# A transformer block on one core: forward sweeps half a step earlier, projections ahead of the scores, one bfloat16 product for a sum of squares

## The chip, the cores and the metric

The kernel runs on one core of a Trainium2 chip. The metric is the device time of one execution in microseconds (us). The engines are named as in the profile: PE multiplies matrices, PEld loads its weights, DVE, ACT and POOL do elementwise work, SP and ACT issue most of the DMAs.

## The reference

One diffusion-transformer block on x[2048, 1024], the first 256 rows of context apart. The input projection feeds eight heads of width 128: four of a gated linear recurrence (HGRN2) and four of retention. Each head runs over the sequence in both directions, its output is normalised per row, gated, and projected back; a gated feed-forward part with a three-tap convolution and a last normalisation follow.

```python
def step(r, inp):                                  # retention, per chunk of 64 rows
    qc, kc, vc = inp
    scores = jnp.einsum('bhtk,bhsk->bhts', qc, kc) * intra
    o = (jnp.einsum('bhts,bhsv->bhtv', scores, vc)
         + jnp.einsum('bhtk,bhkv->bhtv', qc * q_dec[:, :, None], r))
    r_new = (chunk_dec[:, None, None] * r
             + jnp.einsum('bhsk,bhsv->bhkv', kc * k_dec[:, :, None], vc))
    return r_new, o
```

HGRN2 has the same shape with a decay for every column and row in the place of `intra`. Retention's q and k are rotated first (`u1*cos - u2*sin`, `u1*sin + u2*cos`).

## The kernel before

**Products.** Every projection is a scheme of seven block products in the place of eight (`unit`: pa, pb, pa, pc, pa, pc, pa), and each block product is three float16 matmuls of high and low halves (`mm3`, L84 to L86). In the head stages a block product has 24 matmuls: `w_z` (q and k, or q and the forget gates) moves 256 columns per matmul, `w_vg` (values and output gate) 128. In the feed-forward part 512 columns move. After each block product ACT (L545, L547, L585) or DVE (L579) takes the result out of PSUM.

**Heads.** The tokens lie in four groups of 512. `heads()` walks 32 steps (h, i): head h of eight (0 to 3 HGRN2, 4 to 7 retention), group 3 - i. A step has two strands, which `weave` emits alternately: the main strand, `step(h, i)`, and a filler, the projection of the next step (18 block products for HGRN2, 14 for retention; 11 or fewer at the end). `weave` keeps the number of emitted filler pieces in proportion to the main strand's yields.

**Two sweeps.** `step(h, i)` runs the backward recurrence of head h over its group (`hg_sweep1` L809, with seven levels of scores `sc` L833 and DVE scaling L849 between them; or `ret_sweep1`), and beside it the forward recurrence of head h - 1, whose first sweep left all four groups behind. The forward sweep of group i has two parts. `hg_sweep2` or `ret_sweep2`: `fwd_state` makes four matmuls `o` (float32, L901), each followed by a DVE update of the state (L903); DVE adds `o` to the backward part (L928, L929 or L1236); `head_out` takes four sums of squares on ACT (L913), and `rstd` makes 1/sqrt of them in six small POOL instructions (`rs_v` to `rs_y`, L67 to L72). `hg_sweep2b` or `ret_sweep2b`: DVE scales the rows by that (L935 or L1243), four transposes on PE bring the result into `otp` (L920), ACT copies it, and a DMA writes it out. The first part is emitted at the start of the step, the second after the third yield of the main strand.

**Retention's rotation.** At the end of a step's filler for a retention head, ACT and DVE have written k and q side by side into one tile (shown as K). Four DMAs on ACT's queue (L1169) bring a copy with its 32-row blocks swapped (shown as Q). POOL multiplies the copy by sin (L1189), DVE multiplies K by cos (L1192) and adds both (L1193). The next step begins with the scores `rsc` (L1202), four float32 matmuls on that sum; DVE masks them (`rA`, L1204); transposes `rkp` (L1111), the increments `rup` (L1120), `rop` (L1215) and `rob` (L1222) follow.

**Upward weights.** In the feed-forward part `up_weights` is called 22 times. It loads two blocks of weights, takes their squares on ACT (L1478) into bfloat16, which also leaves the row sums in two columns `ssq`, multiplies the squares with a column of ones (16 matmuls of one column, `col`, L1483), and calls `allsum` (L102 to L108): one float32 matmul of one column per column of `ssq` with a square of ones (L107), which leaves the total on all partitions. `scales` (L649) makes the scale of the weights of it.

**Order.** The program is built with `tile.TileContext(nc, schedule_with_timeline_sim=True)`: each engine's order is set by the order of emission, moved by the scheduler's own estimate of when operands are ready. Every engine then executes its list in that order, and a wait holds up what stands behind it on that engine. One instruction (L1192) is held behind another by `issue_after`.

Of the kernel before, what the change touches and what calls it, by code (L numbers as in the profile page):

```python
# [11 lines left out]
BF16 = mybir.dt.bfloat16  # L12
# [3 lines left out]
ALU = mybir.AluOpType  # L16
PSUM = bass.MemoryType.PSUM

P = 128
# [4 lines left out]
NG = SEQ // G  # L24
CT = 256
NH = 4
# [20 lines left out]
def view(t, off, dims):  # L47
    return bass.AP(t.tensor, t.offset + off, [t.ap[0]] + dims)


class Kern:
# [50 lines left out]
    def allsum(self, cols, tag="tu"):  # L102

        o = self.ps(tag, [P, 1], "allsum")
        n = cols.shape[-1]
        for i in range(n):
            self.nc.tensor.matmul(o, self.onesq, cols[:, i:i + 1], start=i == 0, stop=i == n - 1, skip_group_check=True)  # L107
        return o  # L108

    def allmax(self, col, tag="tu"):  # L110
# [827 lines left out]
        nc.scalar.copy(m, tp.rearrange("p c t -> p (c t)"))  # L938
        nc.scalar.dma_start(self.mixd[h][:, g * G:(g + 1) * G], m)

    def weave(self, main, filler, n_main, n_fill):

        done = 0
        for j, _ in enumerate(main):
            while filler is not None and done * n_main < (j + 1) * n_fill:
                done += 1
                if next(filler, self) is self:
                    filler = None
        for _ in filler or ():
            pass  # L950

    def step(self, h, i, W, cur, prev, pr):

        pool = self.mp
        g = NG - 1 - i
        slot = i if h % 2 == 0 else NG - 1 - i
        hg, hgp = h < NH, h - 1 < NH
        if h < 2 * NH:
            main = (self.hg_sweep1 if hg else self.ret_sweep1)(pool, h % NH, g, slot, pr, cur)
        else:  # L960
            main = iter(())
        if prev is not None:
            (self.hg_sweep2 if hgp else self.ret_sweep2)(pool, (h - 1) % NH, i, prev)
        for j in range(3):
            next(main, None)
            yield
            if i == 0 and j == (1 if hg else 0) and h < 2 * NH:
                yield from (self.hg_context if hg else self.ret_context)(pool, h % NH, W, cur)
        if h or i:
            self.tick(self.n_tick)  # L970
        if prev is not None:
            (self.hg_sweep2b if hgp else self.ret_sweep2b)(pool, (h - 1) % NH, i, prev)
        yield from main
        if h or i:
            self.tick(self.n_tick)

    def heads(self):

        nc, pool = self.nc, self.mp
        W, items = self.W0, self.items0  # L980
        self.mod_first()
        items[5][0]()
        place = [self.gate_tile() for _ in range(4)]
        xc = self.load_rows(None, place)
        self.norm_rows(NG - 1, self.x3)
        for _, comp in items[:4]:
            comp()
        self.lower_bounds()
        self.mod1 = self.modulation(self.ep, pool, view(self.sv, V_N1, [[0, 2], [1, 8]]), self.modT[:, :, 8:16],
                                    self.modT[:, :, 0:8], 0, 1.3)  # L990
        ftags = "Kl", "Kl", "qf0", "qf1", "K0", "Q0"
        for _ in self.first_blocks(NG - 1, self.x3, self.places(ftags, "ftmp"), "pj", 1):
            pass
        for _, comp in items[4:]:
            comp()
        for w, dq in W.values():
            nc.vector.tensor_tensor(dq, dq, self.dqx[:, 0:1], ALU.mult)
        prev, items = None, []
        cur = dict(grp={}, sg={})
        pr = {}  # L1000
        first = self.hg_proj(pool, 0, NG - 1, W, pr, cur, True)
        zq = ("z",) * 7 + ("q",)
        rows = lambda g, tags: self.norm_rows(g, self.load_rows(g, [p() for p in self.places(tags, f"x{g}")]))
        x2 = rows(2, zq)
        for _ in self.with_blocks(first, self.first_blocks(2, x2, self.places(ftags, "ftmp"), "tu")):
            pass
        Wn = W
        for s in range(4 * 2 * NH):
            h, i = divmod(s, NG)
            hn, inn = divmod(s + 1, NG)  # L1010
            if i == 0:
                if h < 2 * NH - 1:
                    Wn, items = self.head_weights(h + 1)
                    n = -(-len(items) // 6)
                    if NH <= h < 2 * NH - 1:
                        mods = [it for c in ((4, 5, 6), (7, 8, 9), (10, 11))[h - NH] for it in self.mod_later(c)]

                        pairs = [items[k:k + 2] for k in range(0, len(items), 2)]
                        none = [(None, lambda: None)] * 2
                        items = []  # L1020
                        while pairs or mods:
                            items += (pairs.pop(0) if pairs else none) + (mods[:2] or none)
                            mods = mods[2:]
                        n = 4
                    self.todo += items
                else:
                    items = self.out_weights()
                    self.todo += items[:5]
                    n = 1
                self.n_tick = n  # L1030
            if i == NG - 1:
                while self.todo or self.loaded:
                    self.tick(4)
                if h == 2 * NH - 1:
                    self.todo += items[5:]
            blocks = None
            if s == 0:
                for _ in self.first_blocks(None, self.norm_rows(None, xc), self.places(("A", "A", "Ta", "Kl"), "cftmp", 2), "tu"):
                    pass
                blocks = self.first_blocks(1, rows(1, ("ou1", "ou2", "ou3", "q", "qf2")), self.places(zq, "ftmp"), "pj")  # L1040
            if s == 1:
                blocks = self.first_blocks(0, rows(0, ("ou2", "ou3", "qf2", "gate", "gate", "q")), self.places(zq, "ftmp"), "pj")
            if s == 4 * 2:
                self.ret_consts()
            prn = {}
            nxt = cur if inn else dict(grp={}, sg={})
            if hn < 2 * NH:
                filler = (self.hg_proj if hn < NH else self.ret_proj)(pool, hn % NH, NG - 1 - inn, Wn if inn == 0 else W, prn, nxt, *((True,) if blocks else ()))
                if blocks:
                    filler = self.with_blocks(filler, blocks)  # L1050
            else:
                filler = chain(self.ret_gate(NH - 1, 0, W, cur), self.ret_gate(NH - 1, 1, W, cur))
            self.weave(self.step(h, i, W, cur, prev, pr), filler, (14 if h < NH else 8) + (0 if i else 19 if h < NH else 10),
                       18 if hn < NH else 14 if hn < 2 * NH - 1 else 11 if hn < 2 * NH else 8)
            pr = prn
            if i == NG - 1:
                prev, W, cur = cur, Wn, nxt
        for i in range(NG):
            self.weave(self.step(2 * NH, i, None, None, prev, None), self.ret_gate(NH - 1, i + 2, W, prev) if i < 2 else None, 3, 4)
            if i == 1:  # L1060
                self.mixed_pairs(0)
# [402 lines left out]
    def up_weights(self, j, ty):  # L1464
# [10 lines left out]
        ssq = kp.tile([P, 2], F32, tag="ssqw2", bufs=2, name="ssqw")  # L1475
# [5 lines left out]
        for i in range(2):  # L1481
            for k in range(KT):
                nc.tensor.matmul(col[:, i:i + 1], sqs[i][:, k * P:(k + 1) * P], self.onesb, start=k == 0 and i == 0,  # L1483
                                 stop=k == KT - 1 and i == 1, skip_group_check=True)
        s, neg, dq = self.scales(self.allsum(ssq, "sc"), self.dqx[:, 1:2], ("dqz", "dqvg")[ty])

        if ty == 0:
            tap = kp.tile([P, 2, 3], F32, tag="taps", bufs=2, name="taps")
# [348 lines left out]
```

## Time and profile before

| | |
|---|---|
| device time, median of 3 runs | 2725.51 us (2723.41 to 2730.9) |
| device time of the profiled execution | 2735.92 us |
| span of the profiled execution | 2734.1 us |
| mean granted clock | 0.969 |
| PE busy | 2557.4 us (94%) |
| PEld busy | 1686.3 us (62%) |
| DVE busy | 1821.8 us (67%) |
| ACT busy | 1343.0 us (49%) |
| POOL busy | 779.3 us (29%) |

The busy times are unions of an engine's instruction intervals over the whole span; a PE that is busy is not PE at its highest rate, since its granted clock varies. By the trace, steps of HGRN2 heads fill about 270 to 800 us, steps of retention heads about 800 to 1300 us, and the upward part of the feed-forward about 1550 to 2263 us. The profiled execution was 10.4 us longer than the median run.

### The profile page before, as it was taken

Reading aid. Unit: us, or ns where it says so; the run is one execution under the profiler, and the core shown is the slowest. Engines: PE = TensorE matmul, PEld = TensorE weight load, DVE = VectorE, ACT = ScalarE, POOL = GpSimd, SP = SyncE. Lnnn points to the kernel's source line nnn. Section 1 sums busy time; section 2 is a strip of 40 time slices with the busy share of each in tenths; the row PEclk is TensorE's granted clock in tenths of the full one; section 3 lists DMA queues with packets and bytes.
Section 4 is the critical chain, followed back from the end, with each engine's and each line's share of the span. In section 5 each row is a group of like instructions: output and inputs, shape, how many; then the busy total and the mean of one; then the engine's idle time right before and its main releaser. Section 6 shows DMA issues by size and latency. Waiting matters only on the chain.

```text
span 2734.1 us, 56424 instructions
## 1 busy us (share of the span) xinstructions
PE 2557.4 (94%) x22829; PEld 1686.3 (62%) x22829; DVE 1821.8 (67%) x3569; ACT 1343.0 (49%) x2902; POOL 779.3 (29%) x905
## 2 busy tenths in 40 slices
PE   5788999999999999988999899999999999999998
PEld 2578888889888888887445344444444444444443
DVE  4988677776757565546464888877877777423553
ACT  4776456564544444435454566555555554411120
POOL 3733112220313132221244344334433433000101
PEclk6799999999999999999999999999999999999999
DMA  8224334243447676766631133333233234734552
GB/s 282 115 86 156 103 110 135 93 132 115 144 132 255 207 238 198 241 184 196 211 110 62 57 121 104 108 112 113 99 105 116 89 112 163 268 143 172 205 194 100
DMA packets 216694, 402.39 MB, mean 147 GB/s; under 512 B 16623, under 2 KB 98771, under 8 KB 211824
## 3 DMA queue, kind: packets, MB, share of 16 engines
q1 hardware_dynamic: 203808, 373.42, 39.8%
q10 hardware_dynamic: 12320, 25.18, 3.0%
q8 instruction: 179, 2.93, 0.4%
q14 instruction: 83, 0.68, 0.1%
q0 software_dynamic: 304, 0.17, 0.0%
HBM read 298.57 MB, written 91.75 MB: 143 GB/s over the span
## 4 chain that ended last, share of the span: by engine, by line
PE 61%; DVE 15%; DMA 8%; issue 7%; ACT 4%; POOL 4%; ACTq 1%; SPq 0%; POOLq 0%; DVEq 0%
PE pa L84 6%; PE pa L85 6%; PE pa L86 6%; PE pd L86 5%; PE pd L84 5%; PE pd L85 5%; DMA Q<-K 3%; PE pc L84 3%; PE pc L85 3%; PE pc L86 3%; PE pb L84 2%; PE pb L86 2%; PE pb L85 2%; PE opp L84 2%; PE opp L85 2%
## 5 line engine op out<-in xcount | busy, mean ns | idle before, releaser
L84 PE MATMUL pa<-feat,w 128*128 128x512 f16 x704 | 268.4, 381 | 14.2 <-ACT ta L545 9.8
L85 PE MATMUL pa<-feat,w 128*128 128x512 f16 x704 | 268.1, 381 | 0.0
L86 PE MATMUL pa<-feat,w 128*128 128x512 f16 x704 | 264.9, 381 | 0.0
L86 PE MATMUL pd<-wd,actl 128*128 128x512 f16 x616 | 233.5, 379 | 0.0
L85 PE MATMUL pd<-wd,actl 128*128 128x512 f16 x616 | 233.5, 379 | 0.0
L84 PE MATMUL pd<-wd,actl 128*128 128x512 f16 x616 | 232.8, 379 | 0.0
L85 PEld LDWEIGHTS <-w 128*128 128x128 f16 x1232 | 120.7, 98 | 156.8 <-issue 16.9
L86 PEld LDWEIGHTS <-w 128*128 128x128 f16 x1232 | 121.4, 99 | 145.3 <-issue 1.7
L84 PEld LDWEIGHTS <-w 128*128 128x128 f16 x1232 | 121.5, 99 | 141.4 <-issue 2.0
L85 PEld LDWEIGHTS <-hx 128*128 128x128 f16 x1824 | 182.0, 100 | 9.5 <-issue 7.3
L86 PEld LDWEIGHTS <-hx 128*128 128x128 f16 x1824 | 182.1, 100 | 2.8 <-issue 1.9
L84 PEld LDWEIGHTS <-hx 128*128 128x128 f16 x1824 | 182.4, 100 | 2.3
L1593 DVE SCALAR_TENSOR_TENSOR st<-act,modT,st 128x512 f16<-128x512 f32 x154 | 144.3, 967 | 32.1 <-ACT st L1592 32.1
L1592 ACT ACTIVATE st<-act,modT 128x512 f16<-128x512 f32 x154 | 107.3, 718 | 85.2 <-DVE act L1582 31.4
L84 PE MATMUL pa<-w_vg,hx 128*128 128x128 f16 x800 | 145.2, 222 | 2.9 <-DVE cb L579 2.3
L85 PE MATMUL pa<-w_vg,hx 128*128 128x128 f16 x800 | 144.9, 222 | 0.0
L86 PE MATMUL pa<-w_vg,hx 128*128 128x128 f16 x800 | 144.8, 222 | 0.0
L84 PE MATMUL pc<-feat,w 128*128 128x512 f16 x352 | 133.5, 379 | 1.2 <-ACT feat L1367 1.1
L86 PE MATMUL pc<-feat,w 128*128 128x512 f16 x352 | 133.5, 379 | 0.0
L85 PE MATMUL pc<-feat,w 128*128 128x512 f16 x352 | 133.5, 379 | 0.0
L84 PE MATMUL pa<-hx,w_z 128*128 128x256 f16 x464 | 127.7, 275 | 5.1 <-ACT ct L545 1.6
L85 PEld LDWEIGHTS <-w_z 128*128 128x128 f16 x1072 | 109.2, 102 | 36.4 <-issue 24.1
(550 smaller groups left out, 7563.0 us busy)
## 6 DMA issues: line engine op xcount, KB each, us to landing
hx<-hxd SPq DMA_DIRECT2D x212, 512.0 KB, 4.9
actd<-st SPq DMA_DIRECT2D x154, 256.0 KB, 2.0
actl<-actd SPq DMA_DIRECT2D x28, 1024.0 KB, 5.0
wur<-in_w_up_dram SPq DMA_DIRECT2D x44, 512.0 KB, 3.8
raw<-in_w_in_dram SPq DMA_DIRECT2D x36, 512.0 KB, 4.3
wm<-in_w_mod_dram SPq DMA_DIRECT2D x64, 256.0 KB, 3.8
hxd<-hx SPq DMA_DIRECT2D x28, 512.0 KB, 3.2
wdb<-in_w_down_dram SPq DMA_DIRECT2D x44, 256.0 KB, 4.0
```

The source lines that it names most:

```text
L84: mm(ps, lhs(0), rhs(0), start=start, stop=False, skip_group_check=True)
L85: mm(ps, lhs(0), rhs(1), start=False, stop=False, skip_group_check=True)
L86: mm(ps, lhs(1), rhs(0), start=False, stop=stop, skip_group_check=True)
L1592: nc.scalar.activation(p[:, 0], v, AF.Copy, scale=s)
L1593: nc.vector.scalar_tensor_tensor(p[:, 1], v, s, p[:, 0], ALU.mult, ALU.subtract)
```

## The change

There are three edits.

1. `step`: within a head, the forward sweep of group i + 1 is emitted in step i, its first part after the main strand's third yield, its second part at the end of the step. Group 0's sweep stays at the start of step 0, so that the last step of a head (i = 3) has no forward sweep of its own. The pass behind the last head is as before.
2. `weave` takes `lead`: with retention heads (h >= 4) two block products of the filler are emitted ahead of the main strand's first instruction, which is `rsc`.
3. `allsum16`: in `up_weights` DVE adds the two columns of `ssq` into one bfloat16 column (`both`, L113 of the new kernel), and one bfloat16 matmul (L115) takes the place of the two float32 ones. It is done 22 times: 44 float32 matmuls of one column go, 22 bfloat16 ones and 22 DVE additions come.

```diff
+    def allsum16(self, cols, tag):
+
+        both = self.wp.tile([P, 1], BF16, tag="both", bufs=2, name="both")
+        self.nc.vector.tensor_tensor(both, cols[:, 0:1], cols[:, 1:2], ALU.add)
+        o = self.ps(tag, [P, 1], "allsum")
+        self.nc.tensor.matmul(o, view(self.onesb, 0, [[0, P]]), both, start=True, stop=True, skip_group_check=True)
...
-    def weave(self, main, filler, n_main, n_fill):
-
-        done = 0
+    def weave(self, main, filler, n_main, n_fill, lead=0):
+
+        done = lead
+        for _ in range(lead):
+            next(filler)
...
-        if prev is not None:
-            (self.hg_sweep2 if hgp else self.ret_sweep2)(pool, (h - 1) % NH, i, prev)
+        if prev is not None and (last or i == 0):
+            other(sweep2, i)
         for j in range(3):
...
         if h or i:
             self.tick(self.n_tick)
-        if prev is not None:
-            (self.hg_sweep2b if hgp else self.ret_sweep2b)(pool, (h - 1) % NH, i, prev)
+        if prev is not None and (last or i == 0):
+            other(sweep2b, i)
+        ahead = prev is not None and not last and i + 1 < NG
+        if ahead:
+            other(sweep2, i + 1)
         yield from main
         if h or i:
             self.tick(self.n_tick)
+        if ahead:
+            other(sweep2b, i + 1)
...
-                       18 if hn < NH else 14 if hn < 2 * NH - 1 else 11 if hn < 2 * NH else 8)
+                       18 if hn < NH else 14 if hn < 2 * NH - 1 else 11 if hn < 2 * NH else 8, 2 if h >= NH else 0)
...
-        s, neg, dq = self.scales(self.allsum(ssq, "sc"), self.dqx[:, 1:2], ("dqz", "dqvg")[ty])
+        s, neg, dq = self.scales(self.allsum16(ssq, "sc"), self.dqx[:, 1:2], ("dqz", "dqvg")[ty])
```

**Place 1, POOL, steps of head 4.** `Q<-Q,sin` is the rotation's multiply of one group, the six `rs_` rows are the forward sweep's 1/sqrt of one group (here of head 3). Before:

```order
L1189 TENSOR_TENSOR Q<-Q,sin 128x1024 x2
L67 TENSOR_SCALAR rs_v<-ossq 128x4
L68 TENSOR_TENSOR rs_y<-rs_v,mhalf 128x4
L69 TENSOR_TENSOR rs_t<-rs_y 128x4
L70 TENSOR_TENSOR rs_t<-rs_t,rs_v 128x4
L71 TENSOR_SCALAR rs_t<-rs_t 128x4
L72 TENSOR_TENSOR rs_y<-rs_y,rs_t 128x4
```

The changed kernel at the same place:

```order
L1208 TENSOR_TENSOR Q<-Q,sin 128x1024
L67 TENSOR_SCALAR rs_v<-ossq 128x4
L68 TENSOR_TENSOR rs_y<-rs_v,mhalf 128x4
L69 TENSOR_TENSOR rs_t<-rs_y 128x4
L70 TENSOR_TENSOR rs_t<-rs_t,rs_v 128x4
L71 TENSOR_SCALAR rs_t<-rs_t 128x4
L72 TENSOR_TENSOR rs_y<-rs_y,rs_t 128x4
L1208 TENSOR_TENSOR Q<-Q,sin 128x1024
```

Two multiplies stood ahead of one group of six; now a group of six stands between them, and the two alternate through the steps of retention.

**Place 2, PE, the forward sweep of head 4, group 2 (step h = 5).** `o` are the sweep's matmuls, `rkp` the transposes behind this step's scores, `w_vg` and `hx` the filler. Before, behind the step's scores:

```order
L86 MATMUL pc<-w_vg,hx 128x128
L107 MATMUL allsum<-ssqw,ones 128x1
L901 MATMUL o_15654<-Sf,qf 128x128
L901 MATMUL o_15654<-ou,qf 128x128 x3
L1111 MATMUL rkp<-ident,K 128x128 x4
```

The changed kernel, ahead of the step's scores:

```order
L86 MATMUL pa<-w_vg,hx 128x128
L84 LDWEIGHTS hx
L84 MATMUL pa<-w_vg,hx 128x128
L909 MATMUL o_15381<-Sf,qf 128x128
L909 MATMUL o_15381<-ou,qf 128x128 x3
L85 LDWEIGHTS hx
L85 MATMUL pa<-w_vg,hx 128x128
```

The same four matmuls moved up by some 600 rows of PE's list, from behind the scores into the projection ahead of them. The transposes `otp` of that group moved up by less (from 203 rows behind the matmuls to 604).

**Place 3, PE and DVE, one sum in the upward stage.** `col` is the last of the 16 products with ones, `feat` and the `w` behind it are the projection. PE before:

```order
L1483 LDWEIGHTS w_27837
L1483 MATMUL col<-onesb,w_27837 128x1
L107 MATMUL allsum<-ssqw,ones 128x1 x2
L86 LDWEIGHTS w_27538
L86 MATMUL pb<-feat,w_27538 128x512
```

PE now:

```order
L1502 LDWEIGHTS w_27855
L1502 MATMUL col<-onesb,w_27855 128x1
L115 LDWEIGHTS onesb
L115 MATMUL allsum<-both,onesb 128x1
L84 LDWEIGHTS w_27555
L84 MATMUL pb<-feat,w_27555 128x512
```

DVE now, at the addition of the same sum:

```order
L1587 SCALAR_TENSOR_TENSOR act<-edge,taps,act 128x1
L1582 SCALAR_TENSOR_TENSOR act<-ta,taps,act 128x511
L1588 SCALAR_TENSOR_TENSOR act<-edge,taps,act 128x1
L113 TENSOR_TENSOR both<-ssqw 128x1
L587 TENSOR_TENSOR ta<-pc,ta 128x512
L1581 SCALAR_TENSOR_TENSOR act<-ta,taps,act 128x511
```

On PE the sum keeps its place behind the column products. On DVE the addition `both` stands ahead of the next evacuation of a projection block (`ta<-pc`).

## Rows read from the trace of the kernel before

**Rows 1.** Windows by stage (stretch, length, busy by engine, PEclk, DMA share, GB/s).

```profile
270.00:800.00 530.00, 493.73 (x8095) 443.62 (x8094) 372.35 (x843) 291.39 (x726) 99.16 (x113) 0.98 0.36 119
800.00:1300.00 500.00, 449.37 (x5257) 422.09 (x5257) 302.39 (x675) 223.90 (x565) 118.87 (x143) 0.96 0.66 213
1600.00:2300.00 700.00, 697.26 (x3518) 324.06 (x3517) 559.51 (x964) 408.17 (x717) 282.87 (x188) 1.00 0.31 106
```

**Rows 2.** Waits of PE, whole span (total us, times, longest us).

```profile
PE sc L833 <- DVE Q L849: 13.9, 4, 3.7
...
PE otp L920 <- DVE ou L1243: 12.9, 4, 6.7
...
PE otp L920 <- DVE ou L935: 10.2, 6, 3.0
...
PE rsc L1202 <- DVE K L1193: 7.8, 3, 3.2
...
PE rsc L1202 <- DVE p2t L97: 4.5, 1, 4.5
```

**Rows 3.** Timeline of PE, two waits of `otp` whose place changes little.

```profile
820.63 0.66 PE L920 MATMUL otp<-ident,ou 128*128 128x128 f32 x4 [1.49 <-DVE ou L935]
...
1046.95 0.85 PE L920 MATMUL otp<-ident,ou 128*128 128x128 f32 x3 [3.36 <-DVE ou L1243]
```

**Rows 4.** Timeline of PE at one sum of the upward stage (start, duration).

```profile
1691.45 0.47 PE L1483 MATMUL col<-onesb,w 128*128 128x1 bf16 x13
...
1691.78 0.59 PE L107 MATMUL allsum<-ssqw,ones 128*128 128x1 f32 x4
...
1692.23 0.38 PE L86 MATMUL pb<-feat,w 128*128 128x512 f16 x1
```

**Rows 5.** Timeline of DVE and ACT ahead of the same sum.

```profile
1688.85 0.69 DVE L579 TENSOR_TENSOR ta<-pc,ta 128x512 f32<-128x512 f32 x1 [2.41 <-ACT ta L545]
...
1689.89 0.19 ACT L1478 ACTIVATION_READ_ACCUMULATOR w<-wur 128x1 f32 x1
```

**Rows 6.** Timeline of the forward sweep of head 3, group 3 (step h = 4).

```profile
903.48 0.69 DVE L928 TENSOR_TENSOR ou<-ou,o 128x512 f32<-128x512 f32 x1 [0.83 <-PE o L901]
...
910.82 2.35 POOL L1189 TENSOR_TENSOR Q<-Q,sin 128x1024 f32<-128x1024 f32 x1 [20.52 <-DMA Q<-K]
...
913.25 0.19 POOL L67 TENSOR_SCALAR rs_v<-ossq 128x4 f32<-128x4 f32 x1
...
916.52 1.09 PE L920 MATMUL otp<-ident,ou 128*128 128x128 f32 x4 [2.98 <-DVE ou L935]
```

**Rows 7.** Windows behind three waits of PE (columns as in rows 1).

```profile
882.00:886.00 4.00, 4.00 (x36) 3.86 (x37) 4.00 (x6) 3.46 (x8) 3.00 (x2) 0.64 0.40 138
916.50:922.00 5.50, 5.47 (x32) 4.51 (x33) 5.37 (x13) 3.37 (x9) 0.00 (x0) 0.50 0.46 142
1111.00:1115.00 4.00, 4.00 (x19) 3.27 (x20) 2.19 (x4) 0.84 (x2) 0.00 (x0) 0.50 1.03 413
```

**Rows 8.** Timeline of one rotation and its scores (step h = 6, i = 2).

```profile
1093.99 0.46 ACT L585 ACTIVATE K<-pa,dqk 128x256 f32<-128x256 f32 x1
...
1106.10 3.38 POOL L1189 TENSOR_TENSOR Q<-Q,sin 128x1024 f32<-128x1024 f32 x1 [9.41 <-DMA Q<-K]
...
1110.80 2.08 PE L1202 MATMUL rsc<-K 128*128 128x128 f32 x8 [3.16 <-DVE K L1193]
```

**Rows 9.** Timeline of PE in that step: matmuls of 128, then 256 columns.

```profile
1105.05 0.22 PE L84 MATMUL pa<-w_vg,hx 128*128 128x128 f16 x1
...
1106.06 0.27 PE L84 MATMUL pb<-hx,w_z 128*128 128x256 f16 x1
...
1107.37 0.27 PE L86 MATMUL pa<-hx,w_z 128*128 128x256 f16 x1
```

**Rows 10.** Groups by line and form, DVE: one state update of a forward sweep.

```profile
L903 DVE SCALAR_TENSOR_TENSOR ou<-ou,T 128x128 f32<-128x128 f32 x32 | 11.1, 347 | 0.3
```

**Rows 11.** Timeline of DVE: a multiply that starts within POOL's.

```profile
851.39 3.21 DVE L1192 TENSOR_TENSOR K<-K,cos 128x1024 f32<-128x1024 f32 x1
```

More of the change, by code (lines that the diff above doesn't have):

```diff
@@ L107, in allsum @@
             self.nc.tensor.matmul(o, self.onesq, cols[:, i:i + 1], start=i == 0, stop=i == n - 1, skip_group_check=True)
+        return o
+    def allsum16(self, cols, tag):
[3 more added lines that the diff above has]
+        self.nc.tensor.matmul(o, view(self.onesb, 0, [[0, P]]), both, start=True, stop=True, skip_group_check=True)
         return o
@@ L957, in step @@
         hg, hgp = h < NH, h - 1 < NH
-        if h < 2 * NH:
+        last = h == 2 * NH
+        sweep2, sweep2b = (self.hg_sweep2, self.hg_sweep2b) if hgp else (self.ret_sweep2, self.ret_sweep2b)
+        other = lambda sweep, k: sweep(pool, (h - 1) % NH, k, prev)
+        if not last:
             main = (self.hg_sweep1 if hg else self.ret_sweep1)(pool, h % NH, g, slot, pr, cur)
@@ L966, in step @@
             yield
-            if i == 0 and j == (1 if hg else 0) and h < 2 * NH:
+            if i == 0 and j == (1 if hg else 0) and not last:
                 yield from (self.hg_context if hg else self.ret_context)(pool, h % NH, W, cur)
```

## The prediction

> **What bounds the kernel now.** I read the windows by stage first. In the upward stage PE is busy 697.3 of 700 us at a granted clock of 1.00, DVE 559.5 [rows 1]: what goes from PE there goes from the time. In the HGRN2 steps PE is busy 493.7 of 530 us and DVE 372.4, in the retention steps PE 449.4 of 500 and DVE 302.4 [rows 1]. There PE is the busiest engine, but it stops: what a change is worth is in the waits that end last. So I went on to the list of PE's waits. The transposes of a forward sweep, `otp`, wait 12.9 us for retention's scaled rows and 10.2 us for HGRN2's, ten times in all. The scores of retention, `rsc`, wait 7.8 us for the rotated k and q, and 4.5 us once for a late DVE instruction. The level scores `sc` of HGRN2 wait 13.9 us for DVE [rows 2]. These are the three places that the first two edits touch.
>
> The timeline of one sweep shows why `otp` waits. DVE adds the `o` products at 903.48, `otp` starts at 916.52: 13.0 us. Of these, POOL's six small instructions and DVE's scaling take only 916.52 - 913.25 = 3.3; they stood behind the rotation's multiply, which began at 910.82 when its DMA landed [rows 6]. PE had less than 13 us of other work in its list between the two and stopped for 2.98.
>
> A stop costs more than itself. Behind `otp` at 916.5 the granted clock is 0.50 for 5.5 us, that is 1.2 of 2.4 GHz; behind the stop that ended at 882 it is 0.64 on average over 4 us; behind the score wait that ended at 1110.8, 0.50 over 4 us [rows 7]. Before the fall PE had stood idle in each. At full speed the first two stretches would have taken 5.5 x 0.50 + 4 x 0.36 = 4.2 us less.
>
> **The sums (edit 3).** Two float32 matmuls take 1692.23 - 1691.78 = 0.45 us of PE. A bfloat16 matmul of one column takes (1691.78 - 1691.45) / 13 = 0.025 [rows 4]. The new sum is of the latter kind: 0.45 - 0.025 = 0.425 saved, 22 times **-9.3 us**. Bounds: 0 if PE waits for the operand as long, and -9.9 if even the new one is hidden. Its operand has a new step, DVE's addition `both`, which waits for ACT's sums of squares. ACT had them at 1690.08, PE's sum began at 1691.78 [rows 4, 5], and an addition of two columns is of the size of the smallest DVE instructions. So it comes in time. The addition now stands ahead of the evacuation `ta<-pc` that ran at 1688.85, and would hold it up by 1.2 us, after DVE had been idle for 2.41 [rows 5]. I cost that at nothing: DVE has 140 us to spare in the stage [rows 1], and the block that needs this PSUM bank again is a block product further.
>
> **The earlier sweeps (edit 1).** Four `o` matmuls, six to nine DVE instructions, four squares on ACT, six on POOL, four transposes, a copy and one DMA are moved, none added. I counted PE's instructions between `o` and `otp` in the new order. Prices: a matmul of 128 columns (1106.06 - 1105.05) / 18 = 0.056 us, of 256 columns (1107.37 - 1106.06) / 12 = 0.109 [rows 9]; a float32 one 2.08 / 4 at half clock, so 0.26 [rows 7, 8]. For head 4's group 2 there were 87, 12 and 12 of them, 9.3 us, and now there are 214, 84 and 12, 24.3 us: more than the 13.0 that the slow case of the chain took. Of the ten waits, seven rise like this (from 9 to 11 us of work to 15 to 41). Three don't: the one in the last pass, 6.7, which the edit leaves alone [rows 2], head 3's group 0, 1.49, and head 4's group 3, 3.36 [rows 3], where the distance is as before (14.3 and some 10.2 us). So 12.9 + 10.2 - 6.7 - 1.5 - 3.4 = **-11.5 us** goes; bounds 0 and -16.4 (all but the last pass). On POOL a group of six now stands between each two multiplies, so that the six wait for at most one. Two sweeps, group 1 of heads 4 and 5, get shorter distances (17.3 to 10.1 us): without a multiply ahead of the six, 10 us suffice; with one, each stops for 2.9, which the range holds.
>
> The half-clock stretches at 882 and 916.5 follow two of the waits that go (head 3's groups 2 and 3): **-4.2 us**, bounds 0 and twice that.
>
> The output's copy and DMA move to the end of the step, behind the rotation's four DMAs on ACT's queue, and nobody reads them before the heads are done: nothing. ACT's squares come earlier among evacuations; ACT is busy 291.4 of 530 and 223.9 of 500 us [rows 1]: nothing.
>
> In HGRN2 the moved sweep's DVE work, four updates of 0.347 [rows 10] and two elementwise instructions like the 0.69 of [rows 6], 2.8 us, now falls among the levels of the step, where PE already waits for DVE [rows 2]. Nine sweeps of heads 0 to 2 move. Bounds: -13.9 if those waits vanish, as no sweep opens a step any more, and 9 x 2.8 = +25 if DVE sets the pace throughout. With DVE busy 70% I take a third of one sweep for each of the three heads, **+3 us**, near the row of mean use.
>
> **The lead (edit 2).** From the last q-and-k product to the scores the chain takes 1110.80 - 1093.99 = 16.8 us in one step, of which PE waited 3.16 [rows 8]. In the new order 16 matmuls of 128 columns and 12 of 256 fewer stand between: 0.9 + 1.3 = 2.2 us less cover, and so +2.2 in this step and in the like one of head 5. The 4.5 us wait of head 7's last step [rows 2] gains 4.9 us of cover and goes. Two steps (first of heads 5 and 6) fall from 19 or more to 15 us: +2 each if the chain is as long there. Head 7's first wait loses 1. Together 4.4 - 4.5 - 1 + 4 = **+3 us**; bounds -12.3 (all score waits gone) and +7 with half clock behind two of them.
>
> **Sum.** -9.3 - 11.5 - 4.2 + 3 + 3 = -19. The profiled execution was 2735.9 (span 2734.1 and 1.8 around it), 10.4 above the median of 2725.5. Against the median: **2706 us**. About 0.3%, 8 us, is what a measurement of this kernel can tell from no change.
>
> **Rivals.**
>
> *A, the rotation sets the pace.* The score chain runs through DMA, POOL and DVE and takes its 17 us whether PE is early or not. What the sweeps give back in the retention steps is then waited for at `rsc`: the 2.98 of [rows 6], at most as much for the stop at 882, 12.9 - 6.7 - 3.4 = 2.8 of retention's own, and 4.2 of clock, 13 in all. For it: [rows 8]. Against: only four of sixteen score groups wait now [rows 2]. 2706 + 13 = 2719, 2712 if half.
>
> *B, the sums gain nothing.* `both` sits behind long DVE work, or holds up `ta<-pc` until PE stops. For it: 1.2 us late at its place. Against: the 2.41 us of idle DVE just there [rows 5]. 2706 + 9.3 = 2715.
>
> *C, slower: DVE is the bound among HGRN2's levels.* All nine moved sweeps cost their 2.8 us, +25 in the place of +3, and behind every second the clock falls for 2.1 us (half of the 4.2 above), +9. 2706 - 3 + 25 + 9 = 2737. It decides from the point where a moved sweep costs PE over 2.4 us: (2733.7 - 2703 - 9) / 9. For it: `sc` waits for DVE now [rows 2]. Against: DVE's 372 of 530 us [rows 1].
>
> *D, DVE and POOL block each other.* POOL's multiply takes 2.35 us in [rows 6] and 3.38 in [rows 8], where DVE's multiply had started just before; DVE's takes 3.21 when it starts within POOL's [rows 11]. The moved sweeps of retention, twelve, come nearer to the multiplies; if each meets one and adds 3.38 - 2.35 = 1.03, +12: 2718. Against: most of the moved DVE work lies 7 to 12 us from the multiply in the new order. The Trainium skill, "SBUF — State Buffer", section "Who interferes with whom", says that a DVE instruction with two SBUF inputs and a POOL instruction that reads SBUF exclude each other for a whole instruction, whichever starts first; by that rule such meetings would be paid in full, and the durations here agree in kind.
>
> **Chances.** The forecast 0.60 (2692 to 2717); A 0.17; B 0.07; C 0.10; D 0.06. Faster by over 0.3% (under 2717.3): all of the forecast, 0.05 of A, 0.04 of B, 0.69. Within 0.3%: the rest of A and B, D and a hundredth of C, 0.22. Slower: 0.09. The range, 2690 to 2726, takes in A, B, D and most of the forecast's bounds, and leaves out C and the tail of large gains.
>
> **What would show it.** Right: `otp` waits of about 11 us in all, nearly all in the last pass and two others; the upward stage 9 us shorter with PE as full as before; no stretch of 0.50 at the steps of head 4's groups 2 and 3. A shows as more `rsc` waits on `K`, with longer idle time of POOL for the DMA. B shows as waits of `allsum` for `both`, or of block products for `ta`. C shows as `sc` waits well above 13.9 us and a longer HGRN2 stage. D shows as multiplies above 2.35 us and state updates above 0.35. I am wrong if the upward stage is not shorter, or if the head stages together do not gain.

## The result, and the profile after

The changed kernel takes **2707.65 us** (median of 4 runs, 2706.15 to 2709.88) against 2724.46 for the kernel before, measured beside it (median of 4, 2720.33 to 2730.9). The ratio is 0.994, with a 95% interval of 0.992 to 0.9961: 10.6 to 21.8 us less. The forecast was 2706, 19 us less, within 2690 to 2726.

The windows by stage of the changed kernel, cut as in [rows 1] and with the same columns:

```profile
270.00:800.00 530.00, 496.89 (x8160) 447.36 (x8158) 371.18 (x857) 292.14 (x728) 97.87 (x113) 0.99 0.37 120
800.00:1300.00 500.00, 456.51 (x5295) 421.39 (x5294) 311.67 (x683) 230.71 (x580) 123.88 (x155) 0.97 0.68 219
1600.00:2300.00 700.00, 699.49 (x3497) 320.88 (x3496) 569.68 (x995) 402.32 (x705) 278.61 (x184) 1.00 0.33 113
```

These windows hold more work than those of before, since the stages begin earlier in them. PE is fuller in all three, and the granted clock is 0.01 higher in the two head stages. To compare like with like, the stages have to be cut at instructions. The timeline of PE of the changed kernel has these starts: the fourth `uf` (an HGRN2 step), the first scores of retention, the first product of the output projection, the first column sum of the upward stage, and the first downward product.

```profile
302.34 1.16 PE L877 MATMUL uf<-V,KTt 128*128 128x128 f32 x8
...
791.90 1.06 PE L1221 MATMUL rsc<-K 128*128 128x128 f32 x8
...
1276.40 0.63 PE L84 MATMUL opp<-wo,mp 128*128 128x512 f16 x1
...
1418.02 0.54 PE L1502 MATMUL col<-onesb,w 128*128 128x1 bf16 x16
...
2298.06 1.03 PE L84 MATMUL pd<-wd,actl 128*128 128x512 f16 x4
```

Their differences give the stages HGRN2 (489.6), retention (484.5), output (141.6) and upward (880.0). The same cuts in the profile of every kernel of this study, in us:

| kernel | edits | HGRN2 | retention | upward |
|---|---|---|---|---|
| before | none | 495.3 | 499.6 | 886.8 |
| after | 1, 2, 3 | 489.6 | 484.5 | 880.0 |
| e1_sums | 3 | 495.8 | 493.2 | 875.7 |
| e2_sweeps | 1 | 492.2 | 488.7 | 884.8 |
| e3_lead | 2 | 493.8 | 498.9 | 884.6 |
| e4_sweeps_lead | 1, 2 | 490.4 | 489.7 | 886.4 |
| e5_hg_only | 1 in HGRN2 steps | 490.0 | 493.4 | 886.9 |
| e6_ret_only | 1 in retention steps | 495.8 | 488.9 | 885.9 |
| e7_no_lead | 1, 3 | 489.6 | 490.6 | 880.6 |
| e8_rot_dve | multiply on DVE | 495.0 | 485.9 | 886.6 |
| e9_all_rot | 1, 2, 3, multiply on DVE | 488.8 | 491.7 | 879.1 |
| e10_sums_rot | 3, multiply on DVE | 497.5 | 484.4 | 879.4 |
| e11_no_lead_rot | 1, 3, multiply on DVE | 489.7 | 489.4 | 875.2 |
| e12_hg_sums_rot | 1 in HGRN2 steps, 3, multiply on DVE | 489.3 | 477.5 | 881.0 |

The table also shows what one profile is worth. The HGRN2 column falls into two groups that do not overlap, 493.8 to 497.5 without early sweeps there (six kernels, mean 495.5) and 488.8 to 492.2 with them (eight, mean 489.9). In retention the code of before and of e1_sums is the same, and their profiles differ by 6.4. So of the 26 us between the two profiled spans (2734.1 and 2708.1), where the medians differ by 16.8, some 9 are not the change's; the ratio is the measure of the whole.

PE's waits in the whole span of the changed kernel (total us, times, longest):

```profile
PE sc L841 <- DVE Q L857: 11.1, 6, 3.7
PE otp L928 <- DVE ou L1262: 11.0, 6, 7.0
...
PE rsc L1221 <- DVE K L1212: 6.9, 5, 2.5
...
PE col L1502 <- ACT w L1497: 5.0, 3, 2.7
...
PE otp L928 <- DVE ou L943: 2.9, 2, 2.3
```

Against [rows 2], `otp` waits for the sweep's DVE rows fall from 23.1 to 13.9 us. 8.0 of that is in the last pass (the forward sweep of head 7), where 6.7 stood; everywhere else they fall from 16.4 to 5.9. `rsc` falls from 12.3 to 6.9, `sc` from 13.9 to 11.1. A wait of `col` for ACT's squares, 5.0 us, is new.

### The profile page after: what moved, and what is told of

The parts are those of the page before. It is cut to its first block, busy times and chain, and to the rows that moved or that the text cites. A ratio compares the mean times of both kernels' runs of the same rounds, so it can differ in the third digit from the quotient of the medians.

```text
span 2708.1 us, 56296 instructions
## 1 busy us (share of the span) xinstructions
PE 2538.8 (94%) x22763; PEld 1669.8 (62%) x22763; DVE 1827.9 (67%) x3591; ACT 1342.9 (50%) x2902; POOL 780.4 (29%) x905
## 3 DMA queue, kind: packets, MB, share of 16 engines
q1 hardware_dynamic: 203808, 373.42, 40.2%
## 4 chain that ended last, share of the span: by engine, by line
PE 65%; DVE 15%; DMA 6%; issue 5%; POOL 4%; ACT 4%; ACTq 0%; DVEq 0%; SPq 0%; POOLq 0%
PE pa L84 7%; PE pa L85 7%; PE pa L86 7%; PE pd L86 5%; PE pd L84 5%; PE pd L85 5%; PE pc L84 3%; PE pc L86 3%; PE pc L85 3%; PE pb L84 2%; PE pb L85 2%; PE pb L86 2%; DMA Q<-K 2%; PE opp L86 2%; PE opp L85 2%
```

## The experiments

**Each edit alone, and the first two together.** The four were measured on one chip, beside the same 31 runs of the kernel before.

e1_sums is the kernel before with this line and the new function only:

```diff
-        s, neg, dq = self.scales(self.allsum(ssq, "sc"), self.dqx[:, 1:2], ("dqz", "dqvg")[ty])
+        s, neg, dq = self.scales(self.allsum16(ssq, "sc"), self.dqx[:, 1:2], ("dqz", "dqvg")[ty])
```

> The kernel before with the new sums alone (edit 3). Theory 1, PE is full in the upward stage and each sum gives back 0.425 us: 9.3 us faster than before (ratio 0.9966), at most 10. Theory 2, the operand that DVE adds comes late or holds up DVE, and the gain is lost: within 2 us of before (ratio 0.999 to 1.001).

Measured: ratio 0.9957 (0.9942 to 0.9972), 11.7 us less on 2730.5. Theory 1; the predicted 9.3 lies inside the interval, theory 2 far outside.

e2_sweeps has the new `step`, with the old sums and without the lead:

```diff
+        if ahead:
+            other(sweep2, i + 1)
         yield from main
         if h or i:
             self.tick(self.n_tick)
+        if ahead:
+            other(sweep2b, i + 1)
```

> The kernel before with the earlier forward sweeps alone (edit 1). Theory 1, the waits of otp go and nothing takes their place: 11.5 + 4.2 - 3 = 12.7 us faster (ratio 0.9953). Theory 2, the retention steps are bound by the rotation's chain, and what otp gives back is waited for at rsc as long as no projection product stands ahead of it: within 4 us of before (0.9985 to 1.0), rsc waits of some 15 us in all in the place of 12.3.

Measured: 0.9965 (0.9954 to 0.9976), 9.6 us less. That is three quarters of theory 1's 12.7, which lies at the interval's edge (12.6); theory 2 is out.

e3_lead has the lead alone:

```diff
-                       18 if hn < NH else 14 if hn < 2 * NH - 1 else 11 if hn < 2 * NH else 8)
+                       18 if hn < NH else 14 if hn < 2 * NH - 1 else 11 if hn < 2 * NH else 8, 2 if h >= NH else 0)
```

> The kernel before with the two projection products ahead of the scores alone (edit 2). Theory 1, the prediction's term: 3 us slower to no change (1.000 to 1.001). Theory 2, the products cover the rotation's chain: the 12.3 us of rsc waits mostly go, 6 to 12 us faster (0.9955 to 0.998).

Measured: 1.0016 (1.0005 to 1.0027), 4.4 us more. Theory 1 has the sign, but not the reason. PE's waits in this run:

```profile
PE otp L928 <- DVE ou L1253: 15.7, 5, 6.5
...
PE otp L928 <- DVE ou L943: 9.2, 7, 2.4
...
PE otp L928 <- DVE modT L243: 5.5, 2, 3.0
...
PE rsc L1212 <- DVE p2t L97: 2.9, 1, 2.9
PE rsc L1212 <- DVE K L1203: 2.2, 3, 1.1
```

The score waits did fall, from 12.3 to 5.1 us, as theory 2 says, and `otp` rose to 30.4 us, from 23.1 in [rows 2] and 1.5 more on `modT`. So with sweeps that start late, two products ahead of the scores mostly move the stop. Together these waits fall by 1.4 us, though, and the profiled run (2730.8 us) is one of the fastest of its twelve (median 2734.5): where the 4.4 us go is not shown.

e4_sweeps_lead is both:

> Earlier sweeps and lead, with the old sums (edits 1 and 2). Theory 1: 12.7 - 3 = 9.7 us faster (0.9964), so that the sums add 9.3 to it in the changed kernel. Theory 2, only the two together help: 9 us faster or more here, though the runs with each alone show little.

Measured: 0.9961 (0.995 to 0.9972), 10.6 us less, theory 1's 9.7 within it. Beside the early sweeps the lead moves the time by 0.0004, which the intervals cannot tell from nothing.

**Where the early sweeps gain.** A switch limits the early order to some steps. The next four kernels were measured on one chip, beside the same 23 runs of before.

```diff
+        early = h < NH
...
-        if prev is not None and (last or i == 0):
+        if prev is not None and (not early or i == 0):
...
-        ahead = prev is not None and not last and i + 1 < NG
+        ahead = prev is not None and early and i + 1 < NG
```

> The kernel before with earlier sweeps in the steps of HGRN2 heads alone (heads 0 to 2 swept early, 9 sweeps). Theory 1, as the prediction has it: three small otp waits go (3.2 us) and DVE's levels take about as much back: 0.999 to 1.001. Theory 2, the gain of edit 1 lies here: 6 us or more faster (under 0.998). Theory 3, DVE is the bound among the levels: slower, over 1.002.

Measured: 0.9986 (0.9977 to 0.9995), 3.8 us less, between theories 1 and 2. The HGRN2 stage is 5.5 us under the mean of the late kernels. PE's waits in that stage, before:

```profile
PE sc L833 <- DVE Q L849: 10.2, 3, 3.4
...
PE otp L920 <- DVE ou L935: 3.2, 3, 1.9
PE sf L840 <- DVE Q L849: 2.8, 1, 2.8
PE kp L864 <- DVE K L844: 1.9, 2, 1.4
```

and in the changed kernel (in e5_hg_only the same three rows read 9.0, 3.1 and 1.1):

```profile
PE sc L841 <- DVE Q L857: 7.4, 5, 2.0
...
PE kp L872 <- DVE K L852: 3.1, 2, 1.6
...
PE sf L848 <- DVE Q L857: 1.1, 1, 1.1
```

The window of the stage, columns as in [rows 1], before:

```profile
302.00:797.30 495.30, 463.96 (x7633) 417.18 (x7632) 346.56 (x794) 271.73 (x683) 90.93 (x108) 0.98 0.37 120
```

and after:

```profile
302.30:791.90 489.60, 461.42 (x7632) 415.23 (x7632) 341.51 (x794) 271.44 (x683) 89.64 (x108) 0.99 0.37 122
```

All three `otp` waits are gone, and of `sc` and `sf` 4.5 us too; `kp` took 1.2. As many matmuls kept PE busy 2.5 us less, as the granted clock is 0.99 in the place of 0.98. So the levels' waits on DVE became shorter, not longer. DVE's busy time in the stage fell by 5.0 us with as many instructions: single ones became shorter, above all the 72 scalings of the levels (58.8 us before, 55.5 now). Why they did stays open.

For e6_ret_only the switch reads `early = NH <= h < 2 * NH`.

> The kernel before with earlier sweeps in the steps of retention heads alone (heads 3 to 6 swept early, 12 sweeps). Theory 1: otp waits of 8 us and their half-clock stretches go, 8 to 12 us faster, nearly all of what edit 1 alone gave (0.9965): 0.9956 to 0.997. Theory 2, given back at rsc: within 3 us of before (0.999 to 1.0).

Measured: 0.999 (0.9981 to 0.9998), 2.7 us less: theory 1 is out, and theory 2's bounds hold. Its waits in the retention stage:

```profile
PE otp L928 <- DVE ou L1263: 10.4, 5, 6.9
PE rsc L1222 <- DVE K L1213: 6.8, 6, 3.0
...
PE allsum L107 <- ACT wo L1304: 4.6, 1, 4.6
PE rsc L1222 <- DVE p2t L96: 3.7, 1, 3.7
...
PE otp L928 <- DVE ou L943: 1.8, 2, 1.2
```

`otp` outside the last pass stands at 4.6 us in the place of 13.2 ([rows 2] less the 3.2 of HGRN2). But 10.5 us of `rsc` waits stay, and an `allsum` of the output weights (`wo`) waits 4.6 us for ACT, which no list of before shows. The time between the first scores of one head and the next tells where it goes: head 4 took 125.7 us before and 122.1 here; head 5 128.5 and 119.1 (from 922.9 to 1051.4 and from 919.9 to 1039.0); head 6 took 121.9 before, 117.6 in e1_sums and 122.9 here; head 7 to the output projection 123.6, 121.7 and 124.8. The gain comes in heads 4 and 5. That part of it goes back in heads 6 and 7 is not shown, since before and e1_sums, with the same retention code, lie over 4 us apart in head 6. The two halves together, 3.8 + 2.7, are less than the 9.6 of edit 1 in one piece, though their intervals (up to 6.3 and 5.2) allow it; that they help each other was not shown.

e7_no_lead is the changed kernel without the lead.

> The changed kernel without the two products ahead of the scores (edits 1 and 3). Theory 1, the lead is worth nothing beside the earlier sweeps, as edits 1 and 1 with 2 came out alike: 0.9925 to 0.995, level with the changed kernel's 0.994 or 2 us faster. Theory 2, the lead is needed: above 0.9955. The upward stage should show whether the col waits at its start, 5.0 us in the changed kernel, come with the sums or with the lead.

Measured: 0.9946 (0.9934 to 0.9957), theory 1. The `allsum` on `wo` waits 4.2 us here, as in e2_sweeps, and 0.8 in e4_sweeps_lead: there the lead covers one late sum, with no effect on the whole that shows. `col` waits 3.6 us for ACT's squares, so these waits do not come with the lead. They came with the new sums in five of seven kernels (3.4 to 5.0 us; their upward stage is 880.0 on average). In the two without, e1_sums and e11_no_lead_rot, the stage is 875.4 on average; why these two escape stays open. With the old sums it is 886.0 (seven kernels).

**Is it POOL's queue?** e8_rot_dve takes the rotation's multiply off POOL, in the kernel before:

```diff
-        nc.gpsimd.tensor_tensor(pt, pt, view(sin, 0, [[0, 2], [1, G]]), ALU.mult)
+        nc.vector.tensor_tensor(pt, pt, view(sin, 0, [[0, 2], [1, G]]), ALU.mult)
```

> The kernel before with the rotation's multiply by sin on DVE in the place of POOL, all else as before. Theory 1, that multiply ahead of POOL's six small instructions makes otp wait in the retention steps: otp waits of those steps outside the last pass (13.3 us in all) fall by half or more, and the run is 3 to 10 us faster (0.9965 to 0.999), though DVE has 16 x 1.2 us more. Theory 2, the other links (squares on ACT, DVE's scaling) make the delay: otp waits stay above 10 us and the time is that of before or above.

Measured: 0.9945 (0.9932 to 0.9959), 15 us less, more than theory 1 asked, and as much as all three edits. Outside the last pass the `otp` waits of the retention steps fall from 13.3 to 6.0 us, by more than half, as theory 1 says; in the last pass they rise from 6.7 to 9.7. Head 3's three waits (1.49, 2.54 and 2.98 before) are gone: those were POOL's multiply. Two are left, in the sweep of head 4, groups 2 and 3 (3.35 and 2.63 us, where 1.65 and 3.36 stood). The first of them, on POOL, DVE and PE:

```profile
996.60 0.20 POOL L72 TENSOR_TENSOR rs_y<-rs_y,rs_t 128x4 f32<-128x4 f32 x1
...
1000.23 1.23 DVE L1189 TENSOR_TENSOR Q<-Q,sin 128x1024 f32<-128x1024 f32 x1 [4.75 <-DMA Q<-K]
...
1001.63 1.14 DVE L1243 SCALAR_TENSOR_TENSOR ou<-ou,rs_y,gate 128x128 f32<-128x128 f32 x4
...
1002.13 0.30 PE L920 MATMUL otp<-ident,ou 128*128 128x128 f32 x1 [3.35 <-DVE ou L1243]
```

It is the same multiply in another list. POOL is done with 1/sqrt at 996.80, but the scaling that uses it stands on DVE behind the multiply, which waits there 4.75 us for its DMA. Before, POOL's six stood behind it at this place (it ran from 1003.83, they from 1006.27). The second wait is alike: 1/sqrt is done at 1031.21, the multiply begins at 1033.33.

The score waits fell from 12.3 to 5.6 us. Here a second thing changed: the multiply takes 1.22 or 1.23 us on DVE in all 16 cases, where POOL took 2.35 to 3.42, and POOL no longer meets DVE's long instructions with it (rival D). What of the 15 us is the queue, the shorter chain or the meetings was not separated, and the profiled run (2721.8 us) is the slowest of its six (median 2713.6).

**Both cures at once.** On one chip, beside the same 14 runs of before. The multiply on DVE is the same one-line edit in each.

> The changed kernel (edits 1 to 3) with the rotation's multiply by sin on DVE. Theory 1, the multiply on DVE gains by a shorter rotation and score chain, which the three edits leave as it was: the gains add up, 0.994 - 0.0055 = 0.9885, at most 0.991. Theory 2, both take away the same waits of otp behind POOL's multiply: 0.992 to 0.995.

> The kernel before with the new sums (edit 3) and the multiply on DVE, no earlier sweeps and no lead. Both gains lie in different stages, so they add up: 0.9957 - 0.0055 = 0.990 (0.988 to 0.9925). If edits 1 and 2 are worth their 0.39% beside the multiply on DVE, the run with all three edits is 4 to 10 us faster than this one; if they take away the same waits, the two are level.

> New sums, earlier sweeps and the multiply on DVE, no lead. Theory 1, the lead is worth nothing: level with the run that has the lead too, within 0.001. Theory 2, the lead covers a late scores chain or the late sums of the output weights (4.2 us in the runs without it): 3 to 5 us slower than the run with it.

> New sums, the multiply on DVE, and earlier sweeps in the steps of HGRN2 heads alone. Theory 1, the early sweeps of retention give back in heads 6 and 7 what they gain in head 5, and the multiply on DVE has their gain already: this is the fastest, 0.9875 to 0.990. Theory 2, they add to it: slower than the run with all edits and the multiply on DVE by 2 us or more.

| kernel | ratio | 95% interval |
|---|---|---|
| e9_all_rot | 0.9962 | 0.9949 to 0.9974 |
| e10_sums_rot | 0.9939 | 0.9919 to 0.9959 |
| e11_no_lead_rot | 0.9941 | 0.9925 to 0.9958 |
| e12_hg_sums_rot | 0.991 | 0.9891 to 0.993 |

e9_all_rot missed both theories, on the slow side. A third thing happened. Its timeline of DVE and PE around one stop:

```profile
904.32 1.23 DVE L1208 TENSOR_TENSOR Q<-Q,sin 128x1024 f32<-128x1024 f32 x1 [8.06 <-DMA Q<-K]
905.47 0.34 DVE L911 SCALAR_TENSOR_TENSOR ou<-cs,cd,ou 128x128 f32<-128x128 f32 x1
905.73 0.34 DVE L1243 SCALAR_TENSOR_TENSOR Kt<-rSb,cd,rup 128x128 f32<-128x128 f32 x1
...
906.12 0.49 PE L1241 MATMUL rob<-Kt,K 128*128 128x128 f32 x2 [3.55 <-DVE Kt L1243]
```

DVE stood 8.06 us with the multiply at the head of its list, waiting for the rotation's DMA. Behind it were the updates of the early sweep (L911) and of the backward state (L1243), and PE's `rob` waited 3.55 us for the latter. The list of waits has the sum:

```profile
PE rob L1241 <- DVE Kt L1243: 15.4, 6, 4.1
```

It is 11.9 us in e11_no_lead_rot, and in e12_hg_sums_rot, whose sweeps stay late in retention, 2.7:

```profile
PE rob L1242 <- DVE Kt L1244: 2.7, 3, 1.8
```

So in retention the early sweeps and the multiply on DVE spoil each other: the queue that waits for the DMA changed from POOL to DVE, and the backward state came to stand behind it. Their retention stages are 491.7 and 489.4 us, against 485.9, 484.4 and 477.5 in the three kernels with the multiply on DVE and late sweeps there. e12_hg_sums_rot is the fastest kernel of the study, as theory 1 says, though 0.001 above its bounds: some 24 us under before and faster than e9_all_rot beyond both intervals. Its interval overlaps those of e10_sums_rot and e11_no_lead_rot; against the changed kernel's 0.994 it was not run on one chip, and the intervals overlap by 0.001. e10_sums_rot should have been 0.990 by addition; its interval reaches to 0.9919, and why it falls short, with the upward stage 6.6 us shorter, stays open. Beside the multiply on DVE edits 1 and 2 are not worth their 0.39%: e9_all_rot lies 0.002 above e10_sums_rot, where 4 to 10 us less or a level time was expected, though the intervals overlap. e11_no_lead_rot is 0.002 under e9_all_rot, against theory 2 and a little more than theory 1's 0.001; the intervals overlap.

## Why the prediction was right, point by point

**The sums, -9.3: right in mechanism, given back in part.** One sum in the changed kernel, on PE:

```profile
1747.61 0.16 PE L115 MATMUL allsum<-both,onesb 128*128 128x1 bf16 x1
...
1747.63 0.38 PE L84 MATMUL pb<-feat,w 128*128 128x512 f16 x1
```

From 1747.61 to 1747.63 it takes 0.02 us, where two float32 products took 0.45 [rows 4]. The period of the stage (two calls of `up_weights`) shows the same without a model of PE. Before, the first ten columns of every other sum start at

```profile
1738.41 0.39 PE L1483 MATMUL col<-onesb,w 128*128 128x1 bf16 x10
...
1812.62 0.39 PE L1483 MATMUL col<-onesb,w 128*128 128x1 bf16 x10
```

and in the changed kernel at

```profile
1720.23 0.39 PE L1502 MATMUL col<-onesb,w 128*128 128x1 bf16 x10
...
1793.60 0.39 PE L1502 MATMUL col<-onesb,w 128*128 128x1 bf16 x10
```

74.21 and 73.37 us: 0.84 for two sums, 0.42 each, the term to the hundredth. The whole stage gained only 886.0 - 880.0 = 6 us, though, since at its start, before the period settles, `col` now waits for ACT's squares; in e1_sums and e11_no_lead_rot, without these waits, it gained 10.6. The prediction looked at the sum and not at the column products ahead of it.

Rival B's condition came true and cost little. `both` does stand ahead of an evacuation and makes DVE wait for ACT:

```profile
1746.07 0.16 DVE L113 TENSOR_TENSOR both<-ssqw 128x1 bf16<-128x1 f32 x1 [3.58 <-ACT w L1497]
```

Over the 22 sums DVE idled 40.2 us there, yet no list of PE's waits shows `allsum` waiting for `both`, and the period is exact.

**The `otp` waits, -11.5: right in kind.** They fell by 9.2 us, and by 10.5 outside the last pass, whose own wait the prediction held fixed and which grew by 1.3. The sweep of [rows 6] now reads, on POOL and PE:

```profile
881.41 0.19 POOL L67 TENSOR_SCALAR rs_v<-ossq 128x4 f32<-128x4 f32 x1 [4.12 <-ACT qf L921]
...
891.10 0.64 POOL L72 TENSOR_TENSOR rs_y<-rs_y,rs_t 128x4 f32<-128x4 f32 x1
...
893.00 0.66 PE L928 MATMUL otp<-ident,ou 128*128 128x128 f32 x4 [0.66 <-DVE ou L943]
```

The six instructions no longer wait for a multiply. They take longer, as four weight instructions stand between them in the new order, and the greater distance hides it but for 0.66 us. What was expected to stay did not stay as told: head 3's first group went from 1.49 to 2.28 us, head 4's last from 3.36 to three stops of 1.0, which have another cause (rival D below). The two stops of 2.9 us that were allowed for, in group 1 of heads 4 and 5, did not come.

**The half clock, -4.2: right for its stretches.** Behind that stop the granted clock is now 1.00:

```profile
893.00:898.00 5.00, 5.00 (x57) 4.84 (x58) 1.56 (x4) 3.66 (x7) 0.00 (x0) 1.00 0.77 221
1011.00:1015.00 4.00, 4.00 (x25) 3.06 (x24) 4.00 (x7) 0.25 (x1) 0.00 (x0) 0.53 0.90 286
```

The second row is behind head 4's stops, where it still falls to 0.53. But a fall does not follow every stop: in e1_sums, whose retention code is that of before, `otp` stopped for 3.01 us until 881.15, and the clock was 1.00 over the next 4 us; in the changed kernel it falls to 0.66 from 816 to 821, behind head 3's first stop, where it did not before. So the two stretches that the term counts are in part those of one execution.

**DVE among the levels, +3: wrong sign.** The step that failed is the one that put the sweep's DVE work on top of the levels. It counted nothing for the old place that this work leaves, at the opening of a step and ahead of the levels' DVE instructions; that this is the reason is argued, not shown. The stage gained 5.6 us in the place of the 0 that -3.2 and +3 make. Rival C is out by the same numbers.

**The lead, +3: right in size only where it stands alone, for a wrong reason.** Alone it costs 4.4 us, though the `rsc` waits that were to rise fell. Beside the early sweeps, as in the changed kernel, it costs nothing that can be measured.

**Rival A** was told 0.17. Its sign did not come: `rsc` waits on `K` were 7.8 us before, 6.9 in the changed kernel, 6.2 in e2_sweeps and 6.8 in e6_ret_only. In e6_ret_only the expected 8 to 12 us did come out as 2.7. There 10.5 us of `rsc` waits and the late sum of `wo` are left. Against e1_sums, whose retention code is that of before and whose `rsc` waits are 7.6 us, that would be a part given back; against before itself (12.3) it is not. Why retention gained so little there stays open.

**Rival D** was told 0.06. The rotation's multiplies meet less often: nine of POOL's sixteen took over 3 us before, four do now, and together they fell from 46.9 to 42.3 us, while DVE's by cos rose from 22.6 to 24.9. Head 4's last three stops are of this kind, though. The four scalings ahead of them read before

```profile
1046.54 1.14 DVE L1243 SCALAR_TENSOR_TENSOR ou<-ou,rs_y,gate 128x128 f32<-128x128 f32 x4 [2.30 <-POOL rs_y L72]
```

and in the changed kernel, with the first of four POOL instructions on the next weights beside them,

```profile
1003.60 1.27 POOL L497 TENSOR_TENSOR raw<-raw 128x512 f32<-128x512 f32 x1
...
1003.68 5.37 DVE L1262 SCALAR_TENSOR_TENSOR ou<-ou,rs_y,gate 128x128 f32<-128x128 f32 x4 [0.37 <-POOL rs_y L72]
```

Each scaling ends just behind one of the four. These stops are 3.05 of the 13.9 us of `otp` waits.

**The sum.** That 19 came near the measured 16.8 is in part luck, since errors of opposite sign met: HGRN2 gave 5.6 us where nothing was told, the early sweeps in retention alone gave 2.7 where 8.3 and 4.2 were told, the lead cost nothing in the changed kernel where 3 was told, and the start of the upward stage gave 4.6 back.

## What to carry to other kernels

Where an engine executes its list in order, look for the instruction that waits for a DMA, and ask what stands behind it: here six tiny instructions behind a multiply on POOL, and, after moving the multiply, the scaling of the same sweep or the backward state behind it on DVE. Two cures for one wait need not add up; they may, as here, cost time together, so that each has to be tried beside the other. A saving on an engine that is full is worth its own duration in the steady period, but the start of the stage has to be looked at by itself.

## What was not expected of the hardware

The addition `both` is one column of two operands. Its duration is 0.16 us in eleven of 22 cases, and 1.22 in eight. In those eleven no POOL instruction was running; in the other eleven one with operands in SBUF was, and the addition ended 0.02 to 0.03 us behind it (timeline of the changed kernel):

```profile
1699.05 1.59 POOL L503 TENSOR_TENSOR act<-act 128x512 f32<-128x512 f32 x1
...
1699.45 1.22 DVE L113 TENSOR_TENSOR both<-ssqw 128x1 bf16<-128x1 f32 x1
```

POOL's ends at 1700.64, DVE's at 1700.67: the small instruction waited for the large one's end. This is the lock that the Trainium skill describes in "SBUF — State Buffer", section "Who interferes with whom", and it is plainer here than in the multiplies of the prediction's rival D. In this stage DVE pays for it, and has time to spare.
